# Start-up and values phase of a Strassen-style encoder block on one NeuronCore: ones on TensorE first, the norm's gains as one row, the values' weights split by VectorE and GpSimd, the last values staged in other buffers

## The chip, the cores and the metric

The kernel runs on one NeuronCore of a Trainium2 chip. The metric is the time of one execution on the device in microseconds. The shown time is the median of three runs. One further execution was recorded by the hardware profiler; all rows below come from it.

## The reference, cut to what matters

The input x has 1024 rows of 1024 features. One layer is computed:

```python
h = rmsnorm(x, norm_g[l])                       # x * rsqrt(mean(x*x) + 1e-6) * norm_g
proj = jnp.einsum('bsd,de->bse', h, w_in[l])    # 1024 -> 5632
q, k, v, z_a, u_b, v_b, z_b, g_a, g_b = jnp.split(proj, pts, axis=-1)
y_a = stick_breaking_attention(q, k, v) * silu(z_a)        # 8 heads x 64
y_b = spatial_gating(gelu(u_b), gelu(v_b), ...) * silu(z_b)
merged = sigmoid(g_a) * (y_a @ w_up_a) + sigmoid(g_b) * (y_b @ w_up_b)
x = x + merged @ w_out[l]
return rmsnorm(x, final_norm_g)
```

All products are wanted at nearly float32 precision. The change touches the first norm, the values v (512 columns of the projection) and what follows directly behind them.

## The kernel before, in words

Every product is made of three matmuls in the rounded 32-bit format fp32r: a float32 operand is split into a high part (a cast) and a low part (the operand less its high part), and high*high, low*high and high*low are added up in PSUM. `hi_lo` (L215) does such a split: the cast is `copy` on ScalarE (L159), the subtraction is `tt` on VectorE (L168).

`make_h(i)` (L434) handles 128 rows of x. ScalarE squares them with an accumulated sum (L148), GpSimd adds epsilon and raises to the power -1/2 (`rms_scale`, L182 and L168), VectorE multiplies by this scale and by norm_g, 512 columns at a time (`stt`, L174), TensorE transposes four 128x128 blocks into a PSUM tile `tr` (two buffers), and ScalarE and VectorE bring the parts of it to SBUF. For norm_g, one DMA writes its 1024 numbers to all 128 partitions (L416).

`v_unit(i)` (L477) makes 128 rows of the values: 8 blocks of the contraction by 3 matmuls of 512 columns, 24 in all, in one accumulator (X, Y, Z, o in turn), then a split and two stores from buffers of tag `b` (L486 to L490). The values' weights come in 8 tiles `wv_raw`, and their split is interleaved with the first four `make_h` (L492 to L498). Then follow `v_unit` 0 to 3, `make_h` 4 to 7, `v_unit` 4 to 7 (L499 to L504).

The rest of the projection goes in 20 calls of `project` (L532), each a Strassen scheme of seven products (1, 5, 6, 2, 7, 3, 4 in this order) of 12 matmuls. The right operands T[1] to T[7] are made once: T[1] to T[3] are the split quarters of h, T[5], T[6], T[7] and T[4] are splits (`split_quad`, L506) of the differences t1_raw, t2_raw, b12_raw and t4_raw. The weights of each product are split into two buffers of tag `b`.

The order is made by a planner (`Plan.issue`, L235), a list scheduler with a cost for each operation, 0.5 us from one engine to another, and `tail=5.0` us from the end of a DMA to its users. On each engine, of the operations that are ready, the one with the lowest number starts; the number is the place in the program, plus `pl.offset` (the loads and weight splits of `project` have -9000) on all engines but TensorE. So what is ready goes ahead of what is not. Buffers of one tag are handed out strictly in the order in which the program first names them: `b` has 8 slots, `T` 14, `k` 6, `ak` 4, `a` 7. The result is a fixed order on each engine, and each engine works in that order.

Of the kernel before, what the change touches and what calls it, by code (L numbers as in the profile page):

```python
# [11 lines left out]
F32R = mybir.dt.float32r  # L12
AF = mybir.ActivationFunctionType
ALU = mybir.AluOpType
AX = mybir.AxisListType

P = 128
S = 1024
D = 1024
# [61 lines left out]
def raw_words(v):  # L81

    return v.ap().bitcast(F32) if v.buf.dt == F32R else v.ap()
# [7 lines left out]
class Plan:  # L91
# [10 lines left out]
    def buf(self, tag, shape=(P, 512), dt=F32):  # L102
        return Buf(self, tag, shape, dt)
# [112 lines left out]
        self.copy(hi, src)  # L216
        self.tt(lo, src, hi.f32(), ALU.subtract, eng=eng)

    def load(self, out, dram, queue=None):
        q = queue or self.nc.sync  # L220
        rows = out.box[0][1] - out.box[0][0]
        view = isinstance(dram, View)
        self.add("DMA", out.n * rows * 4 / 360e3 + 0.02,
                 lambda: q.dma_start(out=raw_words(out), in_=dram.ap() if view else dram), [out], [dram] if view else [],
                 tail=5.0)

    def store(self, dram, in_, queue=None):
        q = queue or self.nc.sync
# [105 lines left out]
def hybrid_block(  # L334
# [15 lines left out]
    nc = tc.nc  # L350
# [3 lines left out]
    dram = ctx.enter_context(tc.tile_pool(name="dram", bufs=1, space=bass.MemoryType.DRAM))  # L354
    ps = ctx.enter_context(tc.tile_pool(name="ps", bufs=1, space=bass.MemoryType.PSUM))

    slots = {"T": 14, "k": 6, "r": 5, "ak": 4, "e": 4, "f1": 4, "f2": 6, "a": 7, "b": 8, "os": 2, "s": 16,
             "X": 1, "Y": 1, "Z": 1, "z": 2, "tr": 2, "o": 1}
# [13 lines left out]
    pl = Plan(tc, make_tile, slots, psum_tags)  # L372
    buf = pl.buf

    def cbuf(shape):
        return buf("c", shape)

    ident = cbuf((P, P))
    make_identity(nc, ident.ap())
    ident = ident.all  # L380
# [3 lines left out]
    nc.vector.memset(one.ap(), 1.0)  # L384
    sums = cbuf((P, 16))
    gcol = cbuf((P, 16))
    shift = cbuf((P, 4, P))
    carry = cbuf((P, 64))

    def small(c=1):  # L390
        return buf("s", (P, 16))[:, 0:c]

    def blocks(v, k):
        return v.map(lambda a: a.rearrange("p (k c) -> p k c", k=k))

    def half_of(half):
        return slice(half * 512, half * 512 + 512)

    def rms_scale(ss_in, cols):
        ms = small(cols)  # L400
        pl.ts(ms, ss_in, EPS, None, ALU.add, eng="POOL")
        r = small(cols)
        pl.rsqrt(r, ms, nhalf[:, 0:cols])
        return r
# [4 lines left out]
    xb = [buf("k", (P, D)) for _ in range(8)]  # L409
    gb = buf("T", (P, D))  # L410
    wv_raw = [None] * 8
    for i in range(8):
        if i < 6:
            pl.load(xb[i].all, x[i * P:(i + 1) * P, :])
        if i == 0:
            pl.load(gb.all, norm_g.broadcast_to([P, D]))  # L416
        if i < 4:
            for kt in (2 * i, 2 * i + 1):
                if kt < 7:
                    wv_raw[kt] = buf("a")  # L420
                    pl.load(wv_raw[kt].all, w_v[kt])

    def pair_of(tag="T"):
        return [buf(tag, QUAD, F32R), buf(tag, QUAD, F32R)]

    b11_raw, b21_raw = buf("T", QUAD), buf("T", QUAD)
    hq = {(0, 0): pair_of(), (1, 0): pair_of()}
    wv_hi = [buf("T", QUAD, F32R) for _ in range(2)]
    wv_lo = [buf("f1", dt=F32R) for _ in range(3)] + [buf("f2", dt=F32R) for _ in range(5)]
    b12_raw, t1_raw, t2_raw = buf("T", QUAD), buf("T", QUAD), buf("T", QUAD)  # L430
    hq[1, 1] = pair_of()
    b12 = [[buf("r", dt=F32R) for _ in range(4)], [buf("e", dt=F32R) for _ in range(4)]]

    def make_h(i):  # L434
        half, cs = i // 4, slice((i % 4) * P, (i % 4) * P + P)
        xt = xb[i]
        if i >= 6:
            pl.load(xt.all, x[i * P:(i + 1) * P, :])
        junk = buf("ak", (P, D), mybir.dt.bfloat16)
        ss = small()  # L440
        pl.act(junk.all, xt.all, AF.Square, scale=1.0 / 32, accum=ss)
        r = rms_scale(ss, 1)
        for kq in range(2):
            fs = slice(kq * 512, kq * 512 + 512)
            pl.stt(xt[:, fs], xt[:, fs], r, gb[:, fs], ALU.mult, ALU.mult)
            tr = buf("tr")
            for k in range(4):
                kt = kq * 4 + k
                pl.transpose(tr[:, k * P:(k + 1) * P], xt[:, kt * P:(kt + 1) * P], ident)
            src = blocks(tr.all, 4)  # L450
            if half == 0:
                pl.hi_lo(hq[kq, 0][0][:, :, cs], hq[kq, 0][1][:, :, cs], src)
                pl.copy((b11_raw, b21_raw)[kq][:, :, cs], src)
            elif kq == 0:
                pl.copy(b12_raw[:, :, cs], src)
                for k in range(4):
                    ks = slice(k * P, (k + 1) * P)
                    pl.copy(b12[0][k][:, cs], tr[:, ks])
                    pl.tt(b12[1][k][:, cs], tr[:, ks], b12[0][k][:, cs].f32(), ALU.subtract)
                pl.tt(t1_raw[:, :, cs], src, b11_raw[:, :, cs], ALU.subtract)  # L460
            else:
                pl.hi_lo(hq[1, 1][0][:, :, cs], hq[1, 1][1][:, :, cs], src)
                pl.tt(t2_raw[:, :, cs], src, t1_raw[:, :, cs], ALU.subtract)
                pl.tt(b12_raw[:, :, cs], src, b12_raw[:, :, cs], ALU.subtract)

    def h_block(i, kt):
        half, cs, kq = i // 4, slice((i % 4) * P, (i % 4) * P + P), kt // 4
        if (kq, half) == (0, 1):
            return b12[0][kt % 4][:, cs], b12[1][kt % 4][:, cs]
        q = hq[kq, half]  # L470
        return q[0][:, kt % 4, cs], q[1][:, kt % 4, cs]
# [5 lines left out]
    def v_unit(i):  # L477
        acc = buf(("X", "Y", "Z", "o")[i % 4])
        n = 0
        for kt in range(KT):  # L480
            hh, hl = h_block(i, kt)
            whi, wlo = wv_hi[kt // 4][:, kt % 4, :], wv_lo[kt].all
            for a, b in ((hh, whi), (hl, whi), (hh, wlo)):
                pl.mm(acc.all, a, b, n == 0, n == 23)
                n += 1
        for a in range(2):  # L486
            st = buf("b", (P, 4, P), F32R)
            src = blocks(acc[:, a * 256:a * 256 + 256], 4)
            pl.hi_lo(st[:, :, 0:64], st[:, :, 64:128], src)
            pl.store(v_all[i, :, 4 * a:4 * a + 4, :], st.all)  # L490

    for i in range(4):  # L492
        make_h(i)
        for kt in (2 * i, 2 * i + 1):
            if kt == 7:
                wv_raw[kt] = buf("a")
                pl.load(wv_raw[kt].all, w_v[kt])
            pl.hi_lo(wv_hi[kt // 4][:, kt % 4, :], wv_lo[kt].all, wv_raw[kt].all)  # L498
    for i in range(4):  # L499
        v_unit(i)  # L500
    for i in range(4, 8):
        make_h(i)
    for i in range(4, 8):
        v_unit(i)  # L504

    def split_quad(raws):  # L506
        hi, lo = pair_of()
        for c in range(2):
            if len(raws) == 1:
                cs = slice(2 * c, 2 * c + 2)  # L510
                pl.hi_lo(hi[:, cs, :], lo[:, cs, :], raws[0][:, cs, :])
            else:
                cs = slice(2 * c, 2 * c + 2)
                pl.hi_lo(hi[:, cs, :], lo[:, cs, :], raws[c].all)
        return hi, lo

    t4_raw = [buf("k", (P, 2, 512)) for _ in range(2)]
    for c in range(2):
        cs = slice(2 * c, 2 * c + 2)
        pl.tt(t4_raw[c].all, b21_raw[:, cs, :], t2_raw[:, cs, :], ALU.subtract)  # L520
    T = {1: hq[0, 0], 2: hq[1, 0], 3: hq[1, 1]}
    T[5] = split_quad([t1_raw])
    T[6] = split_quad([t2_raw])
    T[7] = split_quad([b12_raw])
    T[4] = split_quad(t4_raw)

# [305 lines left out]
    for word in ORDER.split():  # L834
        name = word.strip("+0123456789")
        n = int(word[-1])
# [145 lines left out]
    for i in range(8):  # L982
# [7 lines left out]
        r = small()  # L990
# [45 lines left out]
```

## Time and profile before

| | us |
|---|---|
| median of three runs | 759.77 (758.30 to 761.34) |
| the profiled execution, its own time | 759.02 |
| its span in the trace | 757.2 |
| TensorE busy | 733.6 (97%) |
| VectorE busy | 566.4 (75%) |
| ScalarE busy | 433.2 (57%) |
| GpSimd busy | 302.8 (40%) |

In the chain of work that ended last TensorE has 91% of the span. In the 40 slices of the span TensorE is at nine tenths or more in all but the first two and the last one. The engines' names in rows are PE (TensorE's matmuls), PEld (its weight loads), DVE (VectorE), ACT (ScalarE), POOL (GpSimd) and SP (SyncE, which issues most DMAs).

### The profile page before, as it was taken

To read this page: it belongs to the slowest core of one execution; us is meant where nothing else is said; L and a number is where in the kernel's file an instruction comes from. 1 tells how busy PE (TensorE), PEld (TensorE's weight loads), DVE (VectorE), ACT (ScalarE), POOL (GpSimd) and SP (SyncE) were. 2 spreads that over 40 slices of the span, in tenths; PEclk is the share of its full clock that TensorE was granted. 3 is DMA by queue.
4 is the path that set the end of the run, shared out by engine and by line. 5 is a ranking of instruction groups with operands and counts; after the bars stand their busy time and mean duration, and the time that the engine had idled before them with its cause. 6 is when DMAs were issued, how large, how long until landed. Compare 5 with 4: busy or idle time off the path is not lost.

```text
span 757.2 us, 10820 instructions
## 1 busy us (share of the span) xinstructions
PE 733.6 (97%) x3524; PEld 607.8 (80%) x3524; DVE 566.4 (75%) x788; ACT 433.2 (57%) x920; POOL 302.8 (40%) x298
## 2 busy tenths in 40 slices
PE   4998999999999999999999999999999999999996
PEld 3876888888888888888888888888888878888885
DVE  4769544688859877989989898989988999961132
ACT  6645754655747556767666585758765545521122
POOL 1400364598648684553656554340412030013110
PEclk9999999999999999999999999999999999999999
DMA  8512249633344365543556345544988726880022
GB/s 339 189 42 101 81 180 248 205 90 127 110 148 139 123 217 177 131 172 107 161 172 178 102 112 166 161 132 150 290 276 270 242 80 211 283 270 1 29 84 111
DMA packets 69177, 121.31 MB, mean 160 GB/s; under 512 B 7296, under 2 KB 17024, under 8 KB 69120
## 3 DMA queue, kind: packets, MB, share of 16 engines
q1 hardware_dynamic: 67968, 118.52, 49.7%
q10 hardware_dynamic: 1152, 2.10, 0.7%
q8 instruction: 28, 0.46, 0.2%
q14 instruction: 29, 0.24, 0.1%
HBM read 81.27 MB, written 39.32 MB: 159 GB/s over the span
## 4 chain that ended last, share of the span: by engine, by line
PE 91%; DVE 3%; issue 2%; ACT 1%; POOL 1%; DMA 1%; SPq 0%; POOLq 0%; DVEq 0%; ACTq 0%
PE Y L131 24%; PE X L131 24%; PE Z L131 20%; PE z L131 9%; PE o L131 8%; PE tr L135 5%; DVE T L168 1%; DMA k<-in_x_dram 1%; POOL r L168 1%; DVE ak L192 1%; POOL a L168 0%; PE z L135 0%; ACT T L159 0%; DVE b L168 0%; ACT ak L148 0%
## 5 line engine op out<-in xcount | busy, mean ns | idle before, releaser
L131 PE MATMUL Y<-T,b 128*128 128x512 f32 x672 | 180.4, 400 | 2.8 <-ACT b L159 2.0
L131 PE MATMUL X<-T,b 128*128 128x512 f32 x660 | 174.6, 396 | 0.0
L159 ACT CAST b<-a 128x512 fp32r<-128x512 f32 (+1 forms) x152 | 93.3, 616 | 102.2 <-PE Y L131 28.7
L131 PEld LDWEIGHTS Y<-T,b 128*128 128x128 f32 x672 | 123.7, 190 | 27.4 <-ACT b L159 2.4
L131 PE MATMUL Z<-T,b 128*128 128x512 f32 x540 | 145.1, 397 | 0.0
L131 PEld LDWEIGHTS X<-T,b 128*128 128x128 f32 x660 | 121.1, 188 | 23.2
L168 DVE TENSOR_TENSOR b<-a,b 128x512 fp32r<-128x512 f32 (+1 forms) x112 | 102.6, 918 | 45.0 <-ACT b L159 41.6
L131 PEld LDWEIGHTS Z<-T,b 128*128 128x128 f32 x540 | 98.2, 188 | 18.3
L168 POOL TENSOR_TENSOR b<-a,b 128x512 fp32r<-128x512 f32 x40 | 60.1, 1504 | 111.9 <-ACT b L159 63.7
L168 POOL TENSOR_TENSOR f<-f,f 128x512 f32<-128x512 f32 (+1 forms) x38 | 57.1, 1510 | 31.1 <-ACT f L148 20.2
L199 DVE TENSOR_TENSOR_SCAN ak<-ak,c 128x128 f32<-128x128 f32 (+1 forms) x64 | 65.3, 1025 | 3.4 <-ACT ak L148 3.2
L168 POOL TENSOR_TENSOR r<-r,ak 128x512 f32<-128x512 f32 x32 | 44.3, 1395 | 58.3 <-DVE ak L192 28.6
L168 POOL TENSOR_TENSOR a<-a,a 128x512 f32<-128x512 f32 x40 | 59.7, 1493 | 16.3 <-DVE b L168 14.9
L148 ACT ACTIVATE ak<-z 128x128 f32<-128x128 f32 (+2 forms) x96 | 47.1, 493 | 25.7 <-PE z L131 21.9
L131 PE MATMUL o<-e,k 128*128 128x512 f32 (+1 forms) x192 | 60.2, 344 | 0.3 <-ACT e L159 0.2
L131 PE MATMUL z<-k,k 128*128 128x512 f32 (+2 forms) x216 | 59.7, 356 | 0.1
L168 DVE TENSOR_TENSOR e<-tr,e 128x512 fp32r<-128x512 f32 (+1 forms) x96 | 52.3, 546 | 9.8 <-ACT e L159 9.4
L159 ACT CAST e<-tr 128x512 fp32r<-128x512 f32 (+1 forms) x96 | 45.7, 479 | 23.4 <-PE tr L135 17.8
L135 PE MATMUL tr<-c,r 128*128 128x128 f32 x320 | 58.3, 273 | 0.0
L148 ACT ACTIVATE r<-z 128x128 f32<-128x128 f32 (+2 forms) x96 | 47.2, 495 | 11.9 <-PE tr L135 11.4
L192 DVE TENSOR_TENSOR_SCAN ak<-ak,c 128x512 f32<-128x512 f32 x32 | 49.5, 1565 | 0.0
L135 PEld LDWEIGHTS tr<-c,r 128*128 128x128 f32 x320 | 40.7, 140 | 10.7
(216 smaller groups left out, 1145.5 us busy)
## 6 DMA issues: line engine op xcount, KB each, us to landing
d<-f SPq DMA_DIRECT2D x112, 256.0 KB, 2.7
a<-in_w_pairs_dram SPq DMA_DIRECT2D x80, 256.0 KB, 2.8
f<-d SPq DMA_DIRECT2D x72, 256.0 KB, 3.5
k<-d SPq DMA_DIRECT2D x48, 256.0 KB, 5.3
k<-in_x_dram SPq DMA_DIRECT2D x8, 512.0 KB, 7.2
d<-b SPq DMA_DIRECT2D x16, 256.0 KB, 2.3
k<-d SPq DMA_DIRECT2D x8, 512.0 KB, 5.9
a<-in_w_up_dram SPq DMA_DIRECT2D x16, 256.0 KB, 4.7
```

The costliest lines, as they stand in the source:

```text
L131: lambda: self.nc.tensor.matmul(out.ap(), lhsT=lhsT.ap(), rhs=rhs.ap(), start=start, stop=stop, **kw),
L135: self.add("PE", 0.109, lambda: self.nc.tensor.transpose(out=out.ap(), in_=in_.ap(), identity=ident.ap()), [out], [in_, ident])
L148: return self.nc.scalar.activation(out=out.ap(), in_=in_.ap(), func=func, scale=sc, **kw)
L159: lambda: self.nc.scalar.copy(out=out.ap(), in_=in_.ap()), [out], [in_])
L168: self.add(eng, cost, lambda: e.tensor_tensor(out=out.ap(), in0=in0.ap(), in1=in1.ap(), op=op), [out], [in0, in1])
L192: lambda: self.nc.vector.tensor_tensor_scan(out.ap(), in_.ap(), in_.ap(), 1.0 if init is None else init.ap(), op0=ALU.mult, op1=ALU.bypass),
L199: lambda: self.nc.vector.tensor_tensor_scan(out.ap(), in_.ap(), floor.ap(), init, op0=ALU.mult, op1=ALU.max), [out], [in_, floor])
```

## The change

Ones are written to one block of `shift`, and TensorE multiplies them with each other seven times in float32 ahead of everything. norm_g comes as one row to partition 0; two float32 matmuls of one row of ones by this row spread it over the partitions of two PSUM tiles of tag `z`, and `stt` reads it from there. Eight more transposes, whose result nobody reads, follow those of the first rows. The values' weights are loaded in another order (0 and 1 behind the first rows, 2 to 5 behind the second, 6 behind the third), and each is split by a copy on VectorE and a subtraction on GpSimd. The planner counts 2.2 instead of 5.0 us for these loads. `make_h(4)` stands ahead of `v_unit(3)`. The staging of `v_unit` 6 and 7 takes buffers of tag `ak`. T[5], T[6], T[7] are named ahead of t4_raw and T[4], and these last two get the offset -12000.

```diff
-    def load(self, out, dram, queue=None):
+    def load(self, out, dram, queue=None, tail=5.0):
...
+    shift = cbuf((P, 4, P))
+    nc.vector.memset(shift.ap()[:, 0, :], 1.0)
...
-    for i in range(8):
-        if i < 6:
-            pl.load(xb[i].all, x[i * P:(i + 1) * P, :])
+    idle = buf("o")
+    for n in range(7):
+        pl.mm(idle[:, 0:P], shift[:, 0, :], shift[:, 0, :], True, True)
+    START = 2.2
+    g_rows = [buf("z") for _ in range(2)]
+    for i in range(6):
+        pl.load(xb[i].all, x[i * P:(i + 1) * P, :], tail=START)
         if i == 0:
-            pl.load(gb.all, norm_g.broadcast_to([P, D]))
-        if i < 4:
-            for kt in (2 * i, 2 * i + 1):
-                if kt < 7:
-                    wv_raw[kt] = buf("a")
-                    pl.load(wv_raw[kt].all, w_v[kt])
+            pl.load(gb[0:1, :], norm_g, tail=START)
+            for c in range(2):
+                pl.mm(g_rows[c].all, shift[0:1, 0, :], gb[0:1, half_of(c)], True, True)
+        for kt in ((0, 1), (2, 3, 4, 5), (6, 7), ())[i] if i < 4 else ():
+            if kt < 7:
+                wv_raw[kt] = buf("a")
+                pl.load(wv_raw[kt].all, w_v[kt], tail=START)
...
-            pl.stt(xt[:, fs], xt[:, fs], r, gb[:, fs], ALU.mult, ALU.mult)
+            pl.stt(xt[:, fs], xt[:, fs], r, g_rows[kq].all, ALU.mult, ALU.mult)
...
+            if i == 0 and kq == 1:
+                for k in range(8):
+                    pl.transpose(idle[:, 0:P], xt[:, 512:512 + P], ident)
...
-            st = buf("b", (P, 4, P), F32R)
+            st = buf("b" if i < 6 else "ak", (P, 4, P), F32R)
...
-        for kt in (2 * i, 2 * i + 1):
+        for kt in ((0, 1), (2, 3, 4, 5), (6, 7), ())[i]:
...
-            pl.hi_lo(wv_hi[kt // 4][:, kt % 4, :], wv_lo[kt].all, wv_raw[kt].all)
+            hi = wv_hi[kt // 4][:, kt % 4, :]
+            pl.copy2x(hi, wv_raw[kt].all)
+            pl.tt(wv_lo[kt].all, wv_raw[kt].all, hi.f32(), ALU.subtract, eng="POOL")
     for i in range(4):
+        if i == 3:
+            make_h(4)
         v_unit(i)
-    for i in range(4, 8):
+    for i in range(5, 8):
         make_h(i)
...
+    T = {1: hq[0, 0], 2: hq[1, 0], 3: hq[1, 1]}
+    T[5] = split_quad([t1_raw])
+    T[6] = split_quad([t2_raw])
+    T[7] = split_quad([b12_raw])
+    pl.offset = -12000
     t4_raw = [buf("k", (P, 2, 512)) for _ in range(2)]
     for c in range(2):
         cs = slice(2 * c, 2 * c + 2)
         pl.tt(t4_raw[c].all, b21_raw[:, cs, :], t2_raw[:, cs, :], ALU.subtract)
-    T = {1: hq[0, 0], 2: hq[1, 0], 3: hq[1, 1]}
-    T[5] = split_quad([t1_raw])
-    T[6] = split_quad([t2_raw])
-    T[7] = split_quad([b12_raw])
     T[4] = split_quad(t4_raw)
+    pl.offset = 0
```

## Rows read from the trace of the kernel before

**Rows 1.** Windows: length, busy us per engine (instructions), granted clock, DMA share, GB/s.

```profile
core 0: us, PE busy (x) PEld busy (x) DVE busy (x) ACT busy (x) POOL busy (x), PEclk, DMA share, GB/s
0.00:10.00 10.00, 1.97 (x8) 1.57 (x8) 2.23 (x6) 3.25 (x4) 1.49 (x8) 1.00 0.77 284
10.00:20.00 10.00, 6.88 (x30) 5.52 (x31) 7.94 (x13) 9.24 (x20) 1.59 (x4) 1.00 1.03 400
...
60.00:70.00 10.00, 7.99 (x36) 6.32 (x35) 9.93 (x13) 6.79 (x11) 0.00 (x0) 1.00 0.35 131
...
200.00:700.00 500.00, 498.39 (x2433) 413.45 (x2432) 415.16 (x556) 303.43 (x670) 206.61 (x207) 1.00 0.55 171
```

**Rows 2.** Timeline of TensorE, 39 to 76 us: start, length, operation, [idle before, releaser].

```profile
39.74 1.03 PE L135 MATMUL tr<-c,k 128*128 128x128 f32 x8
42.16 0.49 PE L131 MATMUL X<-T,r 128*128 128x512 f32 x1 [1.38 <-ACT r L159]
42.99 0.50 PE L131 MATMUL X<-T,e 128*128 128x512 f32 x1 [0.34 <-DVE e L168]
...
44.03 0.60 PE L135 MATMUL tr<-c,k 128*128 128x128 f32 x4
44.39 0.48 PE L131 MATMUL X<-f,r 128*128 128x512 f32 x1
44.70 0.40 PE L131 MATMUL X<-T,r 128*128 128x512 f32 x1
...
67.42 0.39 PE L131 MATMUL o<-f,T 128*128 128x512 f32 x1
69.81 0.73 PE L131 MATMUL Y<-T,b 128*128 128x512 f32 x2 [2.01 <-ACT b L159]
71.37 4.14 PE L131 MATMUL Y<-T,b 128*128 128x512 f32 x10 [0.82 <-DVE b L168]
75.35 2.93 PE L131 MATMUL Z<-T,b 128*128 128x512 f32 x12
78.11 2.88 PE L131 MATMUL Y<-T,b 128*128 128x512 f32 x12
80.83 2.88 PE L131 MATMUL X<-T,b 128*128 128x512 f32 x12
```

**Rows 3.** Window of 72 to 73 us, columns as in the first group.

```profile
72.00:73.00 1.00, 1.00 (x4) 0.76 (x3) 1.00 (x2) 0.00 (x0) 0.00 (x0) 0.50 0.64 240
```

**Rows 4.** Timeline of all engines, 0 to 25 us.

```profile
5.06 0.19 ACT L148 ACTIVATION_READ_ACCUMULATOR ak<-k 128x1 f32 x1
5.33 0.22 POOL L182 TENSOR_SCALAR s<-s 128x1 f32<-128x1 f32 x1 [4.04 <-ACT ak L148]
5.64 0.57 POOL L168 TENSOR_TENSOR s<-s,c 128x1 f32<-128x1 f32 x1
6.59 1.41 DVE L174 SCALAR_TENSOR_TENSOR k<-k,s,T 128x512 f32<-128x512 f32 x2 [4.81 <-DMA T<-in_norm_g_dram]
7.39 1.97 PE L135 MATMUL tr<-c,k 128*128 128x128 f32 x8 [7.39 <-DVE k L174]
9.18 1.06 ACT L148 ACTIVATE ak<-k 128x1024 bf16<-128x1024 f32 x1 [3.93 <-DMA k<-in_x_dram]
10.23 0.57 ACT L159 CAST T<-tr 128x512 fp32r<-128x512 f32 x1
14.03 1.16 ACT L159 CAST T<-a 128x512 fp32r<-128x512 f32 x2
14.21 1.11 PE L135 MATMUL tr<-c,k 128*128 128x128 f32 x4 [0.69 <-ACT T L159]
14.97 1.20 PE L131 MATMUL X<-T,T 128*128 128x512 f32 x2
16.83 0.80 PE L131 MATMUL X<-T,T 128*128 128x512 f32 x2
```

**Rows 5.** Groups of instructions by form, whole span: count, busy us, mean ns.

```profile
L168 DVE TENSOR_TENSOR f<-a,T 128x512 fp32r<-128x512 f32 x8 | 5.2, 685 | 0.6 <-ACT T L159 0.6
L652 DVE COPY c<-c 128x128 f32<-128x128 f32 x1 | 0.2, 227 | 0.1
L651 DVE MEMSET c<- 128x512 f32 x1 | 0.5, 485 | 0.1
L168 DVE TENSOR_TENSOR b<-X,b 128x256 fp32r<-128x256 f32 x4 | 1.6, 416 | 0.0
L168 POOL TENSOR_TENSOR a<-a,a 128x512 f32<-128x512 f32 x40 | 59.7, 1493 | 16.3 <-DVE b L168 14.9
```

**Rows 6.** Timeline of VectorE, 65 to 72 us.

```profile
65.27 4.78 DVE L168 TENSOR_TENSOR T<-T,T 128x1024 fp32r<-128x1024 f32 x4
69.97 0.74 DVE L168 TENSOR_TENSOR b<-o,b 128x256 fp32r<-128x256 f32 x2
70.63 0.68 DVE L168 TENSOR_TENSOR b<-a,b 128x512 fp32r<-128x512 f32 x1
```

**Rows 7.** Timeline of ScalarE, 68 to 70 us.

```profile
68.60 0.64 ACT L159 CAST b<-o 128x256 fp32r<-128x256 f32 x2
69.13 0.63 ACT L159 CAST b<-a 128x512 fp32r<-128x512 f32 x1
```

**Rows 8.** Timeline of VectorE, 133 us.

```profile
132.97 1.57 DVE L168 TENSOR_TENSOR b<-a,b 128x256 fp32r<-128x256 f32 x1 [2.38 <-ACT b L159]
```

**Rows 9.** Timeline of GpSimd, 133 us.

```profile
132.96 2.72 POOL L168 TENSOR_TENSOR f<-f,f 128x512 f32<-128x512 f32 x2 [1.16 <-DMA f<-d]
```

More of the change, by code (lines that the diff above doesn't have):

```diff
@@ L224, in load @@
                  lambda: q.dma_start(out=raw_words(out), in_=dram.ap() if view else dram), [out], [dram] if view else [],
-                 tail=5.0)
+                 tail=tail)
     def store(self, dram, in_, queue=None):
@@ L386, in hybrid_block @@
     gcol = cbuf((P, 16))
-    shift = cbuf((P, 4, P))
     carry = cbuf((P, 64))
@@ L437, in make_h @@
         if i >= 6:
-            pl.load(xt.all, x[i * P:(i + 1) * P, :])
+            pl.load(xt.all, x[i * P:(i + 1) * P, :], tail=START)
         junk = buf("ak", (P, D), mybir.dt.bfloat16)
@@ L493, in hybrid_block @@
         make_h(i)
-        for kt in (2 * i, 2 * i + 1):
+        for kt in ((0, 1), (2, 3, 4, 5), (6, 7), ())[i]:
             if kt == 7:
                 wv_raw[kt] = buf("a")
-                pl.load(wv_raw[kt].all, w_v[kt])
-            pl.hi_lo(wv_hi[kt // 4][:, kt % 4, :], wv_lo[kt].all, wv_raw[kt].all)
+                pl.load(wv_raw[kt].all, w_v[kt], tail=START)
+            hi = wv_hi[kt // 4][:, kt % 4, :]
+            pl.copy2x(hi, wv_raw[kt].all)
+            pl.tt(wv_lo[kt].all, wv_raw[kt].all, hi.f32(), ALU.subtract, eng="POOL")
     for i in range(4):
+        if i == 3:
+            make_h(4)
         v_unit(i)
-    for i in range(4, 8):
+    for i in range(5, 8):
         make_h(i)
```

## The prediction
> **What bounds the kernel now.** I read the windows by stage first, then TensorE's timeline where it is not full, then the releasers of its waits. From 200 to 700 us TensorE is busy 498.4 of 500 us [rows 1]. There a matmul of 512 columns costs 0.227 us (twelve in 2.72 us, from 78.11 to 80.83) [rows 2], and this change alters none of them. What can be had lies ahead of 75 us, in three places.
>
> First, the start. The first values matmul runs at 14.97 us [rows 4]; until then ScalarE is the full engine (9.24 of 10 us from 10 to 20) [rows 1]. It squares the second rows only when they land (9.18, idle 3.93), it is behind that with the first cast (10.23), and it comes to the first weight tile at 14.03 [rows 4]. TensorE also starts slowly: four matmuls begin between 14.97 and 16.83, in 1.86 us instead of 0.91, and four transposes take 0.76 us to the next start [rows 4] instead of 0.36 [rows 2]. The page's granted clock is 1.00 there [rows 1]; the instructions themselves run at about half pace.
>
> Second, 40.77 to 42.99 us: the transposes of the fifth rows end, and TensorE has no other work until their splits are there, 1.38 + 0.34 = 1.72 us idle [rows 2].
>
> Third, the end of the values. The last values matmul ends at 67.81; the first product of `project` waits 2.01 us for a cast and then 0.82 us for a subtraction, and runs its other ten matmuls in 4.14 us [rows 2] at a granted clock of 0.50, the lower of the two levels (1.2 GHz), to which it fell after those idle stretches [rows 3]. From 67.81 to the next product's start at 75.35 are 7.54 us for 2.72 us of work: 4.82 us lost.
>
> **The change part by part.**
>
> *Staging of the last values.* The cast waited for is at 69.13, right behind the cast of the last values at 68.60 [rows 7], and its subtraction at 70.63 right behind the last values' two (69.97) [rows 6]. Both belong to tag b, whose slots go out in program order: the weights' buffers come after those of the last `v_unit`, which can't be named before that accumulator is full. With `ak` for units 6 and 7 the weights' split stands behind unit 5, some 11 us of TensorE work earlier. This removes the wait and with it the slow clock: -4.8 us. It adds no instruction; `ak` has four slots, last used by the squares long before. What could be late next is VectorE, full in this stretch (9.93 of 10 us) [rows 1], with four splits of T in 4.78 us [rows 6]. But product 5 needs T[5] 2.7 us later, product 6 T[6] another 2.7 us later, and these begin earlier too (next part). I take all 4.8; the lower end, if VectorE is late with T[5], is half of it.
>
> *`make_h(4)` ahead of `v_unit(3)`.* The 24 matmuls of unit 3 (24 x 0.227 = 5.4 us) now lie between the fifth rows' transposes and unit 4, over the chain of two casts and subtractions that left the gap: -1.7 us. The chains of the other rows, and T[5] and T[6] after them, begin some 5 us earlier on VectorE relative to TensorE; that is the cover for the part above.
>
> *norm_g as one row.* 512 KB less in the queue. It stood between the first rows and weights 0 and 1; at 400 GB/s [rows 1] that is 1.3 us. The second rows, which landed at 9.18, should land at 7 to 8 us. The two float32 matmuls have no row. Each lies between 0.63 us (half of the 1.20 of two slow fp32r ones would be 0.60) and four times that, 2.5 us; I take 1.3. With the row there at about 4.3 us they end near 7, when the scale of the first rows is only just there. That hides them; at the upper end `stt` starts 1.5 us late. `stt` with this operand in PSUM I leave at its 0.70 us [rows 4].
>
> *Ones and extra transposes.* The seven float32 matmuls start near 1 us. From 0.25 us each (a transpose, 1.97/8) [rows 4] to 1 us they end between 2.7 and 8; I take 0.5, so 4.5, before the row of norm_g lands. Nothing waits for their result; only at the upper end do they push the rest. What they can give back is the half pace of the start, (1.86 - 0.91) + (0.76 - 0.36) = 1.35 us. But TensorE then idles some 2 us before the first transposes, and in the third place above it fell to the lower level behind such a gap. I take half, -0.7.
>
> *Split of the values' weights.* ScalarE loses eight casts (0.58 each from the 1.16 of two) [rows 4], VectorE eight subtractions of 0.685. VectorE gains eight copies: by the 128x128 copy of 0.227 and the 128x512 memset of 0.485 [rows 5], between 0.23 and 0.69 (a subtraction); I take 0.45. GpSimd gains eight subtractions of 1.3 to 1.5 us [rows 5], 11 us in all, with nothing else to do there but the scales. That is the catch: by the planner's costs the first such subtraction is ready 0.05 us before the first scale, so GpSimd does it first. The weight tile lands near 4.8, is copied by 5.2, and the subtraction ends near 6.6; the scale takes 0.88 more (5.33 to 6.21 now), and `stt` begins at 7.5 to 8.3 instead of 6.59 [rows 4].
>
> From there: `stt` twice 1.4, transposes, cast of the first half near 9.7 (10.23 now). VectorE, in its order, does two more copies and `stt` of the second rows (2.3 us) before the first low part. So the values matmuls run steadily from 12.1 us if no copy waits, from 13.7 if four copies wait 0.4 us each; I take 13.0.
>
> A row bears on these waits: a 256-column subtraction of VectorE, 0.416 us alone [rows 5], took 1.57 us when it began with a GpSimd operation [rows 8, 9]. The row is of two SBUF inputs; no row shows a copy beside GpSimd. The Trainium skill, "SBUF — State Buffer", section "SBUF: two separate sides", says that a VectorE operation in a two-port mode also takes the port pair that it shares with GpSimd, exclusively and for the whole instruction. The row agrees for two inputs, and by the rule for copies too the start would be the first rival's.
>
> **The sum.** From the steady start TensorE needs 191 matmuls, 43.3 us, and 14 groups of four transposes at 0.36 plus 0.31 - 0.23 for the matmul behind each, 0.44 [rows 2], 6.2 us; the other interruptions of the stretch cost now 1.4 us (53.6 from 14.21 to 67.81, less 43.5, 13 x 0.44, 1.72 and 1.3 slow). 13.0 + 43.3 + 6.2 + 1.4 = 63.9, to which I add 0.7 for half of the slow start and 0.2: 64.8, so 3.0 us earlier than 67.81, in which the gap's 1.7 is contained. With the 4.8 behind it the gain is 7.8 us. The profiled execution took 759.02; 759.0 - 7.8 = 751.2. The median of the runs is 0.75 us above that execution, so 752.0.
>
> The new T[4] order (its subtractions first, 2.4 us of VectorE) stands in the covered stretch and I cost it at nothing; T[5] still has about 10 us of TensorE work before it is due. Were that cover gone, 2.4 us.
>
> **The rivals.**
>
> *The start is no earlier.* GpSimd's eight subtractions and VectorE's copies hold each other up: six copies at up to 1.3 us of waiting put the steady start at 15 to 16 us. For: the order on GpSimd, and the 1.57 row. Against: VectorE and ScalarE together lose work. Then 15.7 + 50.9 + 0.9 = 67.5 and only 0.3 us is gained there (the gap's 1.7 spent), 4.8 behind it: 759.8 - 5.1 = 754.7.
>
> *VectorE becomes the bound behind the values.* It is full from 60 to 70 us now. Of 4.8 half comes back as a wait for T[5] or T[6]: 754.4.
>
> *The staging doesn't free the weights' split,* because ScalarE's or VectorE's order holds another late cast ahead of it. Then the 4.8 stay lost: 759.8 - 3.0 = 756.8.
>
> *Slower.* The planner makes a new order for the whole kernel from another start. Between 200 and 700 us VectorE is busy 83% and TensorE waits for only 1.6 us. If the new order puts one subtraction (0.69 to 0.92 us) in front of a due weight split in each of the 18 or so later `project` calls, 12 to 17 us are lost: 764 to 769. It decides from 0.4 us a call, where the gain is used up. Against: the numbers that set the order are the same there, and TensorE has the same work.
>
> **How the numbers follow.** Forecast 0.56, range of its own 749.5 to 753.5. Start no earlier 0.17, VectorE the bound 0.11, staging without effect 0.07, slower 0.09. The range reaches from 748 (start at 11 us, full pace, all 4.8) to 757 (the third rival). A measurement here tells 0.5%, 3.8 us, from no change, so faster is below 756.0: the forecast, the first two rivals but for a little: 0.83; same 0.08; slower 0.09.
>
> **What would show it.** TensorE's timeline: a first values matmul near 10 to 13 us with starts 0.227 us apart from then on; no idle behind the fifth rows' transposes; the first product directly behind the last values matmul, near 65 us, at granted clock 1.00. GpSimd: a 512-column subtraction ahead of the first scale. VectorE: copies near 0.45 us, longer ones where they wait for GpSimd. The windows from 200 us on: the same idle time as now. I am wrong if the idle of the third place stays, if `stt` starts after 10 us, or if TensorE's idle between 80 and 750 us grows by more than 2 us.

## The result, and the profile after

The changed kernel takes 751.47 us (median of four runs, 751.01 to 751.88) against 760.46 us for the kernel before on the same chip (758.3 to 761.34): a ratio of 0.9886 [0.9862, 0.9909]. A second, longer comparison of the same two gave 752.46 against 758.99, 0.9912 [0.9896, 0.9927]. By the medians the gain is 9.0 us in the one and 6.5 us in the other. The profiled execution took 751.01, with a span of 749.2 where the one before had 757.2: 8.0 us less. Executions of 820.52 us (`no_ones`) and of 1032.46 and 1239.83 us (`staging_only`) ran at mean granted clocks of 0.852, 0.675 and 0.561 and are left out of all medians and comparisons.

The windows by stage say where the 8.0 us are not: from 200 to 700 us TensorE is as busy as before (498.39 in [rows 1]). They are at the start, between 40 and 50 us and between 60 and 80 us, where TensorE is now full. (In the 40 slices of the kernel before, TensorE is below nine tenths in the first, the fourth and the last; the fourth reaches from 57 to 76 us.) Columns as in [rows 1].

```profile
10.00:20.00 10.00, 7.87 (x34) 5.78 (x35) 8.77 (x17) 7.18 (x15) 6.88 (x7) 0.74 0.98 359
60.00:70.00 10.00, 10.00 (x46) 8.29 (x45) 9.86 (x15) 7.46 (x11) 1.38 (x1) 1.00 0.49 184
70.00:80.00 10.00, 10.00 (x46) 8.29 (x45) 7.57 (x7) 6.93 (x12) 4.85 (x4) 1.00 0.24 73
200.00:700.00 500.00, 498.31 (x2432) 413.34 (x2431) 411.56 (x555) 297.39 (x662) 201.04 (x203) 1.00 0.55 169
```

TensorE's timeline of the changed kernel (start, length, operation, idle before and its releaser) answers to [rows 2] and [rows 4]:

```profile
1.04 3.36 PE L131 MATMUL o<-c 128*128 128x128 f32 x14 [1.04 <-DVE c L384]
4.32 2.31 PE L131 MATMUL z<-T,c 1*128 1x512 f32 x4
6.94 1.31 PE L135 MATMUL tr<-c,k 128*128 128x128 f32 x8 [0.31 <-DVE k L174]
...
11.47 1.11 PE L135 MATMUL tr<-c,k 128*128 128x128 f32 x4 [1.81 <-ACT T L159]
13.01 0.79 PE L131 MATMUL X<-T,T 128*128 128x512 f32 x1 [0.43 <-DVE T L163]
13.61 1.05 PE L135 MATMUL tr<-c,k 128*128 128x128 f32 x4
14.31 0.78 PE L131 MATMUL X<-T,T 128*128 128x512 f32 x1
14.89 0.57 PE L131 MATMUL Y<-T,T 128*128 128x512 f32 x1
15.69 0.50 PE L131 MATMUL X<-f,T 128*128 128x512 f32 x1 [0.23 <-POOL f L168]
16.03 0.62 PE L131 MATMUL X<-T,T 128*128 128x512 f32 x2
...
33.56 1.04 PE L135 MATMUL tr<-c,k 128*128 128x128 f32 x8
34.35 0.70 PE L131 MATMUL o<-T,T 128*128 128x512 f32 x2
...
64.29 0.39 PE L131 MATMUL o<-f,T 128*128 128x512 f32 x1
64.51 2.88 PE L131 MATMUL Y<-T,b 128*128 128x512 f32 x12
67.23 2.88 PE L131 MATMUL Z<-T,b 128*128 128x512 f32 x12
```

The reader is to see three things. The transposes of the fifth rows (33.56) are followed at once by matmuls of the next unit: the 1.72 us behind them are gone. The first product (64.51) stands directly behind the last values matmul (64.29), and the next one follows 2.72 us later, which is its work alone. And the start moved less than the figure 13.01 suggests: four values matmuls and sixteen useful transposes have begun when the matmul at 16.03 starts, and that same point lay at 16.83 before [rows 4].

So in these two executions the 8.0 us come from four places. The start gives 16.83 - 16.03 = 0.80. The last values matmul started at 67.42 before [rows 2], so a matmul directly behind it would have started at 67.65 (0.227 later); now one does, at 64.51. From 16.83 to 67.65 TensorE needed 50.82 us, and from 16.03 to 64.51 it needs 48.48: 2.34 less, of which 1.72 is the recorded idle of the gap and 0.62 are smaller interruptions. Behind that point the span has left 757.2 - 67.65 = 689.55 before and 749.2 - 64.51 = 684.7 now: 4.85. Together 8.0. The last part is the steady one: in a second profile of the changed kernel, below, the first product starts at 66.14, so 67.65 - 66.14 = 1.5 us are gained ahead of it instead of 3.1, and behind it the same 4.8.

Why the start moved so little is on VectorE's timeline of the changed kernel (columns the same):

```profile
6.14 1.40 DVE L174 SCALAR_TENSOR_TENSOR k<-k,s,z 128x512 f32<-128x512 f32 x2 [4.23 <-POOL s L168]
...
12.54 1.76 DVE L163 CAST T<-a 128x512 fp32r<-128x512 f32 x5
...
15.04 0.88 DVE L163 CAST T<-a 128x512 fp32r<-128x512 f32 x1
...
19.83 1.47 DVE L163 CAST T<-a 128x512 fp32r<-128x512 f32 x1
```

and on GpSimd's:

```profile
5.23 0.22 POOL L182 TENSOR_SCALAR s<-s 128x1 f32<-128x1 f32 x1 [3.93 <-ACT ak L148]
...
8.53 0.22 POOL L182 TENSOR_SCALAR s<-s 128x1 f32<-128x1 f32 x1 [2.42 <-ACT ak L148]
...
13.04 0.63 POOL L182 TENSOR_SCALAR s<-s 128x1 f32<-128x1 f32 x1 [3.62 <-ACT ak L148]
...
14.36 10.59 POOL L168 TENSOR_TENSOR f<-a,T 128x512 fp32r<-128x512 f32 x8
```

GpSimd makes three scales before its first subtraction, which starts only at 14.36 because the copies of the weights start only at 12.54, although weights 0 and 1 should have landed by about 7 us (in `turn_early`, below, which loads them in the same place, their copies run at 5.67 and 6.72, as soon as they land). The first low part is there at 15.69, and that is when the steady run begins.

### The profile page after: what moved, and what is told of

Read it like the earlier page. It is cut to its first block, busy times and chain, and to the rows that moved or that the text cites. A ratio compares the mean times of both kernels' runs of the same rounds, so it can differ in the third digit from the quotient of the medians.

```text
span 749.2 us, 10867 instructions
## 1 busy us (share of the span) xinstructions
PE 737.4 (98%) x3550; PEld 610.7 (82%) x3550; DVE 567.4 (76%) x789; ACT 428.4 (57%) x912; POOL 314.0 (42%) x306
## 4 chain that ended last, share of the span: by engine, by line
PE 94%; DVE 2%; issue 1%; POOL 1%; ACT 1%; DMA 1%; SPq 0%; POOLq 0%; DVEq 0%; ACTq 0%
PE X L131 24%; PE Y L131 24%; PE Z L131 21%; PE z L131 9%; PE o L131 9%; PE tr L135 5%; DVE ak L192 1%; DMA k<-in_x_dram 1%; PE z L135 0%; DVE T L168 0%; POOL r L168 0%; ACT ak L148 0%; DVE ak L199 0%; DVE e L168 0%; POOL a L168 0%
## 5 line engine op out<-in xcount | busy, mean ns | idle before, releaser
L131 PE MATMUL Y<-T,b 128*128 128x512 f32 x672 | 178.6, 397 | 0.0
L148 ACT ACTIVATE ak<-z 128x128 f32<-128x128 f32 (+2 forms) x96 | 47.1, 493 | 26.1 <-PE z L131 21.9
L148 ACT ACTIVATE r<-z 128x128 f32<-128x128 f32 (+2 forms) x96 | 47.2, 494 | 11.7 <-PE tr L135 11.2
```

Of the source, the lines that this page charges most:

```text
L131: lambda: self.nc.tensor.matmul(out.ap(), lhsT=lhsT.ap(), rhs=rhs.ap(), start=start, stop=stop, **kw),
L148: return self.nc.scalar.activation(out=out.ap(), in_=in_.ap(), func=func, scale=sc, **kw)
```

## The experiments

The comparisons tell 2 us or so apart. A finer measure is the span less the point at which the first product could start, directly behind the last values matmul: where nothing is lost behind the values it is 684.6 to 684.9 us, whatever the kernel, so it separates the start of a kernel from the rest.

| kernel | median us | ratio to before | first product could start | span less that |
|---|---|---|---|---|
| before | 758.99 to 760.46 | | 67.65 (starts 69.81) | 689.6 |
| changed | 751.47 | 0.9886 [0.9862, 0.9909] | 64.51 | 684.7 |
| changed, again | 752.46 | 0.9912 [0.9896, 0.9927] | 66.14 | 684.8 |
| two_lines | 752.29 | 0.9911 [0.9896, 0.9926] | 66.23 | 684.6 |
| staging_only, again | 756.69; again 757.28 | 0.9963 [0.995, 0.9976] | 68.71 | 686.8 |
| staging_b | 759.65 | 1.0004 [0.9992, 1.0017] | 66.65 (starts 69.99) | 692.4 |
| h4_later | 762.48 | 1.0048 [1.0033, 1.0063] | 68.30 | 691.5 |
| wv_act | 751.73 | 0.9898 [0.9874, 0.9923] | 65.34 | 684.7 |
| no_ones | 753.04 | 0.9914 [0.9895, 0.9934] | 66.50 | 684.7 |
| no_ones, again | 752.42 | 0.9914 [0.9898, 0.993] | 67.13 | 684.9 |
| gain_bcast | 754.38 | 0.9933 [0.9915, 0.9952] | 67.62 | 685.2 |
| turn_early | 754.39 | 0.9936 [0.9918, 0.9953] | 66.12 | 686.7 |
| start_mixed | 754.36 | 0.9933 [0.9918, 0.9948] | 66.36 | 686.6 |

**Staging undone.** The changed kernel with the last values staged in tag b again:

```
-            st = buf("b" if i < 6 else "ak", (P, 4, P), F32R)
+            st = buf("b", (P, 4, P), F32R)
```

> The changed kernel with the last two values units staged in tag b again, all else kept. Theory (the order in which tag b is handed out makes the first product's weights wait for the last values): the values end at 64.5 us as before, then the first product waits 2 to 3 us and runs at the lower clock; it ends near 72 instead of 67.2, span +4.8, about 756 us. Rival (the rest of the change, the T[4] order and the earlier rows, would have closed the gap anyway): first product within 0.5 us of the last values matmul, 751.5.

The whole gain is gone: 759.65, where 756 was expected. TensorE's timeline of this kernel shows the wait of [rows 2] again, and longer:

```profile
69.99 0.73 PE L131 MATMUL Y<-T,b 128*128 128x512 f32 x2 [3.19 <-ACT b L159]
...
71.97 4.63 PE L131 MATMUL Y<-T,b 128*128 128x512 f32 x10 [0.96 <-DVE b L168]
```

Its window from 72 us shows the lower level of the clock, as [rows 3] did:

```profile
72.00:76.00 4.00, 4.00 (x10) 3.14 (x11) 2.93 (x5) 1.14 (x2) 0.00 (x0) 0.50 0.39 131
```

It loses more than before (692.4 against 689.6), and the timelines of ScalarE and VectorE say why: the casts and subtractions for T[4] (`T<-k`), which the change moves earlier, now stand ahead of the cast and the subtraction that the first product waits for.

```profile
67.16 1.99 ACT L159 CAST T<-k 128x1024 fp32r<-128x1024 f32 x2
...
69.31 1.15 ACT L159 CAST b<-a 128x512 fp32r<-128x512 f32 x2
...
68.95 2.36 DVE L168 TENSOR_TENSOR T<-k,T 128x1024 fp32r<-128x1024 f32 x2
71.23 0.69 DVE L168 TENSOR_TENSOR b<-a,b 128x512 fp32r<-128x512 f32 x1
```

So the staging is what carries the stretch, and by these lines the new T[4] order costs nothing only because the staging covers it; it was not undone by itself.

**The two lines alone.** The kernel before with only the staging and `make_h(4)` moved:

```
-            st = buf("b", (P, 4, P), F32R)
+            st = buf("b" if i < 6 else "ak", (P, 4, P), F32R)
...
     for i in range(4):
+        if i == 3:
+            make_h(4)
         v_unit(i)
-    for i in range(4, 8):
+    for i in range(5, 8):
```

> The kernel before with only two edits: make_h(4) ahead of v_unit(3), and tag ak for the last two values units. Theory (these two places are 1.7 and 4.8 of the 8 us): start as before (first values matmul at 14.97), values end near 66.1, first product directly behind it, about 753.5 us. Rival (without the faster start VectorE is late with the T splits): first product waits again, 756 or more.

752.29, within the error of the whole change (751.47 and 752.46). Its timeline has the same two joints: the first product at 66.23 without idle before it, and 2.72 us to the next product.

```profile
66.23 2.88 PE L131 MATMUL Y<-T,b 128*128 128x512 f32 x12
68.95 2.88 PE L131 MATMUL Z<-T,b 128*128 128x512 f32 x12
```

All other edits together are worth what this comparison can't tell from nothing.

**`make_h(4)` put back.**

```
     for i in range(4):
-        if i == 3:
-            make_h(4)
         v_unit(i)
-    for i in range(5, 8):
+    for i in range(4, 8):
```

> The changed kernel with make_h(4) behind v_unit(3) again. Theory: the gap behind the fifth rows' transposes returns, 1.7 us, values end near 66.2, 753.2 us. Rival (VectorE is then also late with T[5], because the rows' chains start 5 us later): first product or the one after it waits, 754 to 756.

Slower than before: 762.48. Neither the theory nor the rival had it. The gap behind the fifth rows' transposes returns (1.37 and 0.33), the first product still stands directly behind the values (68.30), but 6.8 us are lost further on (691.5 against 684.7). One place of it is in TensorE's timeline of this kernel:

```profile
42.81 0.50 PE L131 MATMUL X<-T,r 128*128 128x512 f32 x1 [1.37 <-ACT r L159]
43.65 0.50 PE L131 MATMUL X<-T,e 128*128 128x512 f32 x1 [0.33 <-DVE e L168]
...
195.22 0.38 PE L131 MATMUL o<-e,b 128*128 128x256 f32 x1 [2.84 <-ACT e L159]
```

and its windows show TensorE at 6.78 of 10 us there, at a granted clock that falls to 0.83 in the mean. From 200 to 700 us it has 1.4 us more idle than the changed kernel (496.95 us busy).

```profile
190.00:200.00 10.00, 6.78 (x26) 5.26 (x25) 5.42 (x8) 6.04 (x11) 5.02 (x5) 0.83 0.31 108
```

A later start of four chains makes the planner choose another order, and part of the loss lies more than 100 us further on. This is of the kind of the prediction's slower rival, a new order that leaves TensorE waiting, though not its form, one subtraction ahead of a weight split in each call. The changed kernel doesn't have it.

**The staging alone.** The kernel before with the one line of the first experiment reversed.

```
-            st = buf("b", (P, 4, P), F32R)
+            st = buf("b" if i < 6 else "ak", (P, 4, P), F32R)
```

> The kernel before with one edit: tag ak for the last two values units. Theory: the gap behind the fifth rows' transposes stays (1.7 us), the values end at 67.8, the first product follows directly, 4.8 us gained: about 754.3 us. Rival (as in the run with make_h(4) later: the two edits are not independent, the planner's order further on changes and TensorE waits in the middle): product directly behind the values but 2 to 6 us more idle after 100 us, 756 to 760.

756.69: only 2.6 us below the kernel before in the same comparison (759.25). One more execution was recorded:

> The kernel before with tag ak for the last two values units, once more for its profile. Its median was 2.4 us below before where 4.8 were expected. Theory: the first product does follow the values directly, at 67.8, and TensorE waits about 2 us more somewhere between 70 and 700 us. Rival: the first product still waits for its weights.

757.28 in that one execution. The first product starts at 68.71 with no wait, so the 4.8 us are gone from their place. But 686.8 - 684.7 = 2.1 us are lost a little later, on TensorE's timeline:

```profile
91.77 3.01 PE L131 MATMUL X<-T,b 128*128 128x512 f32 x12 [1.14 <-DVE f L168]
95.26 0.73 PE L131 MATMUL Z<-T,b 128*128 128x512 f32 x2 [0.48 <-ACT b L159]
```

TensorE waits there for VectorE to read an accumulator, VectorE waits for ScalarE, and the chain ends on ScalarE's timeline: it loads an activation table (`ACT_TABLE_LOAD`) right ahead of the activation that is due.

```profile
88.43 0.62 ACT L159 CAST b<-a 128x512 fp32r<-128x512 f32 x1
89.07 1.28 ACT L148 ACT_TABLE_LOAD   x1
90.36 1.15 ACT L148 ACTIVATE f<-f 128x512 f32<-128x512 f32 x2
...
91.03 0.69 DVE L168 TENSOR_TENSOR f<-f,X 128x512 f32<-128x512 f32 x1 [1.64 <-ACT f L148]
```

Every kernel here has this load once behind the values; what differs is where the planner's order puts it. In `staging_only` three pairs of activations (L148, L153) run ahead of it, in the changed kernel one (the load is at 77.85), in `two_lines` two (82.16), and in these two TensorE is busy all 40 us from 60 to 100. `turn_early` and `start_mixed`, below, have three pairs ahead of it too, the same wait, and the same 2 us lost. No run moves the load alone, so this cause is read from timelines.

VectorE's splits of T are not the cause, though some of them take twice the 1.21 us of others while GpSimd subtracts:

```profile
74.20 1.21 DVE L168 TENSOR_TENSOR T<-T,T 128x1024 fp32r<-128x1024 f32 x1
...
77.05 2.30 DVE L168 TENSOR_TENSOR T<-T,T 128x1024 fp32r<-128x1024 f32 x1
```

In `two_lines` two such splits take as long, beside the same three GpSimd subtractions, and no wait of TensorE follows:

```profile
74.86 4.55 DVE L168 TENSOR_TENSOR T<-k,T 128x1024 fp32r<-128x1024 f32 x2
```

In `staging_only` itself the products start 2.72 us apart from 68.71 to 87.75, so none of them waited for its T. The rival "VectorE the bound behind the values" is therefore not what happens; the rival of the expectation, another order further on, is. The two edits together give 6.8 us (759.09 - 752.29), the staging alone 2.6: they don't add, since with the staging alone the planner's order on ScalarE is another one.

**The values' weights split by ScalarE and VectorE again.**

```
-            pl.copy2x(hi, wv_raw[kt].all)
-            pl.tt(wv_lo[kt].all, wv_raw[kt].all, hi.f32(), ALU.subtract, eng="POOL")
+            pl.hi_lo(hi, wv_lo[kt].all, wv_raw[kt].all)
```

> The changed kernel with the values' weights split as before (ScalarE casts, VectorE subtracts). Theory (the split is held by the order in which tag T is handed out, not by ScalarE's load: its copies start at 12.5 us in the changed kernel): first low part of the weights about as late as now, values end within 1 us of 64.5, 751 to 752.5 us. Rival (ScalarE's eight casts were the limit of the start): values end 2 us later or more, 753.5 and above.

751.73, the first product at 65.34, between the two profiles of the changed kernel (64.51 and 66.14). GpSimd's part in the split is worth nothing that shows.

**Without ones and extra transposes.**

```
-    for n in range(7):
-        pl.mm(idle[:, 0:P], shift[:, 0, :], shift[:, 0, :], True, True)
...
-            if i == 0 and kq == 1:
-                for k in range(8):
-                    pl.transpose(idle[:, 0:P], xt[:, 512:512 + P], ident)
```

> The changed kernel without the seven ones matmuls and without the eight extra transposes. Theory (the granted clock had fallen to 0.50 by 8.7 us, before the first values matmul, so they give nothing): first values matmul and end of the values within 0.3 us of 13.0 and 64.5, 751.5 us. Rival (the early work brings the clock back sooner, at 15.3 us): the values end 0.7 to 1.3 us later, 752.2 to 752.8.

The first product starts 2.0 us later (66.50), but the times don't follow as clearly: 751.81 to 753.06. So both kernels were run again, side by side.

> The changed kernel, unaltered, on the same chip as the next two. Every theory: 751 to 752 us, ratio to before 0.988 to 0.991. It shows how much the granted clock and the landing of the second rows differ from one execution to another: values end at 64.5 in the first profile; 64.5 again if the start is fixed by the order, up to 2 us later if it hangs on when the clock rises.

> The changed kernel without the ones and the eight extra transposes, as in no_ones, in more rounds. Theory now (the ones bring the clock to its upper level by 4 to 8 us, which shortens the two gain matmuls from 3.75 to 2.0 to 2.3 us and the first transposes, though it falls again): 1 to 2 us slower than after_again in the median. Rival (the 2 us of the one profile were chance): within 0.5 us of after_again.

752.46 with the ones, 752.42 without: no difference that shows. The 2 us between the single profiles lie within the spread between executions of one kernel, and the profiled ones are not the middle ones (751.01 is the fastest of its four, 753.75 the second slowest of its six). The second profile of the changed kernel itself shows it; its order at the start is the same, its pace is not:

```profile
4.33 3.78 PE L131 MATMUL z<-T,c 1*128 1x512 f32 x4
...
16.49 1.05 PE L131 MATMUL X<-T,T 128*128 128x512 f32 x2
```

The gain matmuls take 3.78 us instead of 2.31, and from 16.49 us the matmuls start 0.42 us apart instead of 0.227, at this granted clock:

```profile
17.00:19.00 2.00, 2.00 (x6) 1.46 (x5) 1.92 (x3) 0.00 (x0) 2.00 (x3) 0.50 0.88 286
```

Its first product starts at 66.14, 1.63 us later than in the first profile of the same kernel. With the ones the gain matmuls take 1.98 to 2.31 us in three profiles and 3.78 in four; without them they take 3.75 in both. So the ones raise the pace early in some executions only, and they don't decide at which level of the clock the values run.

**norm_g broadcast by the DMA again**, in the changed kernel:

```
-            pl.load(gb[0:1, :], norm_g, tail=START)
-            for c in range(2):
-                pl.mm(g_rows[c].all, shift[0:1, 0, :], gb[0:1, half_of(c)], True, True)
+            pl.load(gb.all, norm_g.broadcast_to([P, D]), tail=START)
...
-            pl.stt(xt[:, fs], xt[:, fs], r, g_rows[kq].all, ALU.mult, ALU.mult)
+            pl.stt(xt[:, fs], xt[:, fs], r, gb[:, fs], ALU.mult, ALU.mult)
```

> The changed kernel with norm_g spread by one DMA over 128 partitions as before, and no matmuls for it. Theory (512 KB in front of the second rows): these land near 9.2 instead of 7.3, the second scale and with it VectorE's first low part come 1.5 to 2 us later, values end near 66, 752.8 us. Rival (the two gain matmuls at half pace cost as much as the DMA): same as changed, 751.5.

754.38, 1.9 to 2.9 us above the changed kernel, and the second rows' scale comes at 10.36 instead of 8.53. Yet `two_lines` has the broadcast too and takes 752.29. So the row is worth some 2 us in the changed start, and the rest of the new start, without it, costs about as much. Which part costs it stays open: in the kernel with the row neither the ones nor the GpSimd split moves the time, and the new order of the loads and the planner's new landing times were not tried apart.

**The order that the prediction assumed.** The first two weight splits named before the first rows' splits, so that their T buffers come first:

```
+    split_wv((0, 1))
     for i in range(4):
         make_h(i)
-        for kt in ((0, 1), (2, 3, 4, 5), (6, 7), ())[i]:
+        split_wv(((), (2, 3, 4, 5), (6, 7), ())[i])
```

> The changed kernel with the split of weights 0 and 1 named ahead of make_h(0), so that tag T no longer holds it; GpSimd then has two subtractions ahead of the first scale, as the prediction took it to be. Theory of the prediction (each costs 1.3 us, the scale comes at 7.9 instead of 6.1, but the values' matmuls are fed earlier): stt of the first rows at 8 to 8.5, steady values matmuls from 13 to 14 instead of 16, values end 1 to 2 us earlier, 750 us. Rival (the rows' chain is what counts, and it is now 2 us later): values end 1 to 2 us later, 752.5 to 753.5.

The timeline of all engines shows GpSimd's subtractions at 6.18 and 7.80, ahead of the first scale, as the prediction had it for the changed kernel:

```profile
5.67 0.43 DVE L163 CAST T<-a 128x512 fp32r<-128x512 f32 x1 [3.77 <-DMA a<-in_w_v_dram]
6.18 1.26 POOL L168 TENSOR_TENSOR f<-a,T 128x512 fp32r<-128x512 f32 x1 [4.89 <-DVE T L163]
...
7.80 1.26 POOL L168 TENSOR_TENSOR f<-a,T 128x512 fp32r<-128x512 f32 x1 [0.36 <-DVE T L163]
...
9.15 0.28 POOL L182 TENSOR_SCALAR s<-s 128x1 f32<-128x1 f32 x1
...
10.31 1.41 DVE L174 SCALAR_TENSOR_TENSOR k<-k,s,z 128x512 f32<-128x512 f32 x2 [0.46 <-DMA a<-in_w_v_dram]
```

So it was T's turn that kept them back: with the turn changed the copies start at 5.67 instead of 12.54. (This edit also moves the copies forward in the planner's numbers. `start_mixed`, below, leaves these and changes the turn, and there they start at 8.80.) It helps nothing at the start: VectorE's queue now waits for weights to land, `stt` begins at 10.31 instead of 6.14, the first values matmul at 14.45, and the first product starts at 66.12, as in the second profile of the changed kernel. Yet 754.39 is 2 to 3 us worse than the changed kernel. These are lost behind the values (686.7 against 684.7), in the wait of `staging_only`, again right behind the table load (86.30):

```profile
89.00 3.02 PE L131 MATMUL X<-T,b 128*128 128x512 f32 x12 [0.96 <-DVE f L168]
```

**A try at a better start.** T's turn to the weights, low parts alternating between VectorE and GpSimd, and later landing times in the planner's costs:

```
-        pl.load(xb[i].all, x[i * P:(i + 1) * P, :], tail=START)
+        pl.load(xb[i].all, x[i * P:(i + 1) * P, :], tail=START if i == 0 else 4.4)
...
-                pl.load(wv_raw[kt].all, w_v[kt], tail=START)
+                pl.load(wv_raw[kt].all, w_v[kt], tail=4.6)
...
+    wv_hi[0].order, wv_hi[1].order = 1, 2
+    pl.tag_count["T"] = 3
...
-            pl.tt(wv_lo[kt].all, wv_raw[kt].all, hi.f32(), ALU.subtract, eng="POOL")
+            pl.tt(wv_lo[kt].all, wv_raw[kt].all, hi.f32(), ALU.subtract, eng="POOL" if kt % 2 else "DVE")
```

> The changed kernel with tag T handed to the weights' high parts first, the low parts of the even weight tiles subtracted on VectorE and of the odd ones on GpSimd, and the planner told that weights and later rows land later (so the first rows keep their place). Theory (the values' matmuls now wait for the weights' split, which tag T holds to 12.5 us): first values matmul near 10.7, steady from 12 to 13 instead of 16, values end near 62.5, 749.5 us. Rival (the rows' chain through ScalarE and VectorE limits the start anyway): values end at 64 to 65, 751.5; or the new order costs idle further on, 753 and above.

754.36, as the second half of the rival had it. The first values matmul is early, and TensorE then waits 2.67 us for the first rows' own subtraction, which stands behind the copies:

```profile
11.42 0.75 PE L131 MATMUL X<-T,T 128*128 128x512 f32 x1
14.83 0.50 PE L131 MATMUL X<-T,T 128*128 128x512 f32 x1 [2.67 <-DVE T L168]
```

Still its first product starts at 66.36, within half a microsecond of the changed kernel's second profile. The rest is lost behind the values (686.6), at 89.24, in the same wait as in `turn_early`. So neither run says that its start is worse than that of the changed kernel, only that it is no better. No version here beats the changed kernel.

## Why the prediction was right, and where it was not

The forecast of 752.0 us stands beside 751.47 and 752.46, and its sum of 7.8 us beside 8.0 by the profiles and 9.0 and 6.5 by the medians. The two large terms, 4.8 and 1.7, were right in mechanism. Of the other 1.3 us, which were to come from the start, no run shows anything: `two_lines` has none of the new start and takes 752.29. Step by step:

- *Staging, -4.8.* Right in place and size: 4.85 by the spans; undone, it costs 7.7 (692.4 - 684.7), as T[4]'s casts and subtractions then stand in the way. What the prediction feared for it, VectorE late with T[5] or T[6], is in no run. Without the earlier chains of `make_h(4)`, which it named as the cover, 2.1 us come back, near its half of 4.8, but by ScalarE's table load: the price of that rival was met by luck, not by its mechanism.
- *`make_h(4)`, -1.7.* Right: the idle of 1.38 and 0.34 is gone, and returns when the line is put back. Undersized all the same, as the line is worth more than its gap. Taken out of the changed kernel it costs 10 to 11 us, 6.8 of it behind the values in another order of the planner. That can't be read from the profile of before.
- *norm_g as one row.* The second rows landed at 7.30 (forecast 7 to 8, before 9.18), and the two gain matmuls end at 6.63 (forecast near 7): right in the first profile. In the second they end at 8.11, and the second half of the first `stt` waits 0.79 us for them, a delay that the prediction put at the upper end of its bounds.
- *Ones.* They end at 4.40 (forecast 4.5). Half of the slow pace given back was forecast; the runs show nothing that can be told from zero.
- *Split of the values' weights.* This step failed. "By the planner's costs the first such subtraction is ready 0.05 us before the first scale, so GpSimd does it first": it didn't; the first subtraction runs at 14.36, behind three scales, and `stt` begins at 6.14, not at 7.5 to 8.3. The prediction applied the rule that a tag's buffers go out in the order in which they are named to tag b, and overlooked that the weights' high parts are buffers of tag T, named behind the last one that ScalarE fills from the first rows. `turn_early` and `start_mixed` show it.
- *Steady start at 13.0.* Wrong for that reason: 16.03 in the first profile, 3.0 later. The values still ended at 64.51, where 64.8 was forecast, because less was left from there. By the later start more had been done: 188 matmuls and 12 groups of transposes were left where 191 and 14 were taken (0.7 and 0.9), so 1.6 of the 3.0 are not lost time. The other 1.4 were more than made up by luck: 0.5 of other interruptions instead of 1.4 (48.48 - 188 x 0.227 - 12 x 0.44), and none of the 0.9 that the sum adds for slow pace and rest. In the second profile, with slow pace at 17 us, the values end at 66.14, 1.3 late. The first rival had the start right (15 to 16 us), for another reason, and the end wrong by 3.
- *T[4] order at nothing.* Right as long as its cover is there: `two_lines`, with the old T[4] order, has the same 684.6 behind the values. In `staging_b` the cover isn't there, and 2.8 us more are lost than before (692.4 - 689.6), where 2.4 was given.
- *VectorE's copies at 0.45.* They take 0.35 each while GpSimd runs no subtraction (five in 1.76 us at 12.54) and 0.85 to 1.47 while it does. The copy at 19.83 ends at 21.30, some 0.3 behind the end of a GpSimd subtraction (an estimate: the eight take 10.59 us from 14.36, so the fifth ends near 20.98). The Trainium skill, "SBUF — State Buffer", section "SBUF: two separate sides", states that of a GpSimd operation and a VectorE operation in a two-port mode or with two SBUF inputs, whichever starts first keeps the shared port pair for its whole instruction, and the other is blocked. These rows agree, now for copies with one input too. No end hangs on it: TensorE waits for a copy once, 0.43 us at 13.01, and for one of the fast ones.

## What to carry to other kernels

In a kernel whose order is made by a planner with buffers given out in turn, look for every tag that a moved step writes, not only for the tag of the wait that is to go: the turn, not readiness, decided when the weights' copies ran. Judge edits by pairs: of two that were priced at 1.7 and 4.8 us the larger alone gave 2.6 of their 6.8, and taking either out of the changed kernel took the whole gain away. Follow a wait along its chain to the engine where it ends: in `staging_only` VectorE looks late, but the chain of the 2 us ends at a table load of ScalarE. Split the span at a point that all versions share, as the start of the first product: it told a start that is no better from a loss some 23 us later. And when a sum meets the measured time, compare its intermediate points as well: here the end of the values came out within 0.3 us from a steady start that was wrong by 3.

## What the runs showed of the hardware that was not expected

- The start of one and the same kernel differs by 1.6 us between two executions (first product at 64.51 and 66.14) with the same order of instructions: the two gain matmuls take 2.31 us in one and 3.78 in the other, and at 17 to 19 us the granted clock is 1.00 in the one and 0.50 in the other.
- A float32 matmul appears as two instructions: seven of 128 columns as x14 (3.36 us), two of 512 columns with one row as x4.
- VectorE's split of 1024 columns takes up to 2.3 us beside a GpSimd subtraction, and 1.21 otherwise. In `two_lines` that cost TensorE nothing.
- A row's granted clock can read 1.00 while TensorE runs at half pace: in `no_ones` the row of 17 to 19 us reads 1.00, and matmuls from 16.94 us start 0.43 us apart. So near the start the pace has to be read from the starts themselves.
- The one `ACT_TABLE_LOAD` behind the values takes 1.28 us on ScalarE in every version. The three versions with three pairs of activations ahead of it lose 2 us in the first `project` calls; the changed kernel and `two_lines`, with one and two, lose nothing there.
